# Sample rows' scores against their own new keys: one 128 x 128 product, or four blocks of 32 x 32

## The chip, the cores and the metric

The kernel runs on one core of a Trainium2 chip. The metric is the time of one execution on the device in microseconds (us), the median of several runs; lower is better.

## The reference, cut to what matters

A two-layer trunk is stepped once, for a prompt of 256 tokens and for 8 running streams ("samples") of 16 new tokens each, so 3 blocks of 128 rows. Layer 0 has 8 forgetting-attention heads (fox) and 8 stick-breaking heads (sb), head width 128. A sample's token attends to the 128 cached rows of its own stream and to those of its own 16 new tokens that are not after it:

```python
def fox_core(q, k, v, Fq, Fk, qpos, kpos):
    s = jnp.einsum('bqhd,bkhd->bhqk', q, k).astype(jnp.float32) * ATTN_SCALE
    s = s + (Fq - Fk)          # per head, shapes aligned
    s = jnp.where(kpos[None, :] <= qpos[:, None], s, -jnp.inf)
    p = jax.nn.softmax(s, axis=-1)
    return jnp.einsum('bhqk,bkhd->bqhd', p.astype(v.dtype), v)

def sb_core(q, k, v, qpos, kpos):
    z = jnp.einsum('bqhd,bkhd->bhqk', q, k).astype(jnp.float32) * ATTN_SCALE
    before = kpos[None, :] < qpos[:, None]
    log_stay = jnp.where(before, jax.nn.log_sigmoid(-z), 0.0)
    after = lax.cumsum(log_stay, axis=3, reverse=True) - log_stay
    a = jnp.where(before, jnp.exp(jax.nn.log_sigmoid(z) + after), 0.0)
    return jnp.einsum('bhqk,bkhd->bqhd', a.astype(v.dtype), v)
```

Each head's output is multiplied by a SiLU gate and goes through an output projection to the residual. Layer 1 is a gMLP with spatial gating; the change does not touch it. Everything is float32.

## The kernel before

**Dense projections.** Every large product (`dense_nat`, `products`, L93 to L119) has 128 x 512 tiles of weight streamed from DRAM by the SP queue. ScalarE rounds a tile to a high part (`whi`, L84), VectorE makes the low part by subtraction (`wlo`, L86), and TensorE runs three products for each of the three row blocks (L100, L101, L102). `whi` and `wlo` have four buffers each. The input projection of layer 0 is walked in four "quads" of four heads (`quad(g)`); quads 0 and 1 are fox, 2 and 3 are sb.

**Attention between the dense products.** A head's work is a generator (`head`, L605) that is stepped at fixed places in the dense products of the quad and the next one (`places`, L515, put in through `between`). Heads go in pairs. `scores(pair)` (L480) makes the scores of both heads, runs the softmax or the stick-breaking weights, writes the weights to DRAM (L671, ScalarE's queue) and reads them back in blocks of 32 x 32 moved to their transposed place (L496, GpSimd's queue). `attended(pair)` (L501), one dense product later, turns these blocks with a VectorE transpose (`PT`, L674), multiplies them with the values on TensorE and applies the gate. A tile scheduler orders the instructions of each engine by its own estimate of when they are ready; `tc.issue_after` holds some of them behind others.

**One head on TensorE**, all in float32, where the trace shows one product as two records:
- L630, L631: prompt scores, 128 x 128 stationary.
- L633: sample rows against all 128 new keys of all samples, one 128 x 128 product. A mask of -1e30 leaves each stream its own 16 keys.
- L636: sample rows against cached keys, four products with 32 columns of the array each (32 tokens, 256 cached keys), K = 128.
- L681: sample weights of new keys times new values, four products with K = 128 rows and 32 columns.
- L685: the same for cached values, eight products of that form.
- L687 to L689: prompt weights times values, 128 x 128.

So a sample row has T = 384 weights: 256 for cached keys (two streams' slots) and 128 for new keys. A head's tile `weights` (tag `pr`) holds 384 prompt and 384 sample columns, 768 in all, which is six blocks of 128 in DRAM (`wd`).

**Setup.** L310 to L324 make the masks `mp` (prompt) and `md` (sample) for both kinds of heads. For a fox head L610 to L620 add the forget sums to the masks on GpSimd.

Of the kernel before, what the change touches and what calls it, by code (L numbers as in the profile page):

```python
# [8 lines left out]
F32 = mybir.dt.float32  # L9
F32R = mybir.dt.float32r  # L10
AF = mybir.ActivationFunctionType
ALU = mybir.AluOpType
# [3 lines left out]
P = 128  # L16
# [3 lines left out]
T = NT * P  # L20
# [17 lines left out]
def tile_hybrid_step(  # L38
# [7 lines left out]
    nc = tc.nc  # L46
    V, S, G, PE = nc.vector, nc.scalar, nc.gpsimd, nc.tensor
# [5 lines left out]
    dram = ctx.enter_context(tc.tile_pool(name="dram", bufs=1, space=bass.MemoryType.DRAM))  # L53
# [5 lines left out]
    def nm(s):  # L59
        n_names[0] += 1  # L60
        return f"{s}_{n_names[0]}"

    def slot(dt=F32R):
        return slots.tile([P, 4 * T], dt, tag="slot", name=nm("slot"))
# [91 lines left out]

    with ExitStack() as l0:
        lc = l0.enter_context(tc.tile_pool(name="l0c", bufs=1, reuse_waits="tile"))  # L160
        lp = l0.enter_context(tc.tile_pool(name="l0p", bufs=2, reuse_waits="tile"))
# [126 lines left out]
        def select(ap, pattern, base, cm, fill=0.0, op=ALU.is_ge):  # L288
            G.affine_select(out=ap, in_=ap, pattern=pattern, compare_op=op, fill=fill, base=base, channel_multiplier=cm)
# [20 lines left out]
        for strict in (0, 1):  # L310
            mp = lc.tile([P, T], F32, name=f"mp{strict}")
            V.memset(mp, 0.0)
            for j in (1, 2):
                select(mp[:, j * P:(j + 1) * P], [[-1, P]], -strict, 1, NEG)
            md = lc.tile([P, T], F32, name=f"md{strict}")
            V.memset(md, 0.0)
            for s in range(2):
                with late():
                    V.tensor_scalar(out=md[:, s * P:(s + 1) * P], in0=md[:, s * P:(s + 1) * P], scalar1=slotb[:, s:s + 1], scalar2=None, op0=ALU.add)
            mdn = md[:, 2 * P:].rearrange("p (b q) -> p b q", q=16)  # L320
            select(mdn, [[-16, 8], [0, 16]], 0, 1, NEG)
            select(mdn, [[16, 8], [0, 16]], 15, -1, NEG)
            select(mdn, [[-16, 8], [-1, 16]], -strict, 1, NEG)
            masks.append((mp, md))  # L324


# [5 lines left out]
        nFd = dram.tile([8, T], F32, name="nFd")  # L332
# [135 lines left out]
        def quad(g):  # L468
# [5 lines left out]
            own = {"d": dram.tile([4, T, P], F32, name=nm("d"))}  # L474
# [5 lines left out]
            def scores(pair):  # L480

                for hh in pair:
                    hs = slice(hh * P, hh * P + P)
                    own[hh] = head(g, h0 + hh, own["k"][:, hh], lambda hs=hs: own["v"][:, :, hs], own["q"][:, hh],
                                   keys_of[4 * g + hh], lambda n=4 * g + hh: values_of[n], lambda hs=hs: own["z"][:, :, hs])
                wd = own[pair] = dram.tile([2, 6, P, P], F32, name=nm("wd"))
                for hh in pair[::-1]:
                    next(own[hh])
                with tc.issue_after(last_product[0]):
                    for hh in pair:  # L490
                        next(own[hh])
                for j, hh in enumerate(pair):
                    own[hh].send(wd[j])
                blk = own["blk", pair] = slot(F32).rearrange("p (j x) -> p j x", j=2)
                for j in range(4):
                    G.dma_start(blk[32 * j:32 * j + 32].rearrange("p j (a d) -> p (j a) d", d=32),  # L496
                                wd[:, :, :, 32 * j:32 * j + 32].rearrange("j x (a p) d -> p (j x a) d", p=32))
                for hh in pair:
                    cached_keys(4 * g + hh + 2)
# [78 lines left out]
            for tb in range(NT):  # L578
                z, a = zn[:, tb, :], sg[:, tb, :]
# [22 lines left out]
        def tmp(tag, bufs=2, shape=None):  # L602
            return lp.tile(shape or [P, T], F32, tag=tag, bufs=bufs, name=nm(tag))

        def head(g, h, kT, values, qT, kc, vc, gate):  # L605
            fox = g < 2
            mp, md = masks[0 if fox else 1]
            if fox:

                fb = lp.tile([P, 2, T], F32, tag="fb", name=nm("fb"))  # L610
                fc = lp.tile([P, P], F32, tag="fc", bufs=1, name=nm("fc"))
                G.dma_start(fb[:, 0, :2 * P], nFd[h, :2 * P].partition_broadcast(P))
                G.dma_start(fb[:, 0, 2 * P:], nFd[h, :P].partition_broadcast(P))
                G.dma_start(fb[:, 1, 2 * P:], nFd[h, 2 * P:].partition_broadcast(P))
                G.dma_start(fc, nFcd[:, h, :].unsqueeze(1).broadcast_to([8, 16, P]))
                G.tensor_tensor(out=fb[:, 0, :], in0=fb[:, 0, :], in1=mp, op=ALU.add)
                G.tensor_tensor(out=fb[:, 1, 2 * P:], in0=fb[:, 1, 2 * P:], in1=md[:, 2 * P:], op=ALU.add)
                G.tensor_tensor(out=fb[:, 1, :2 * P].rearrange("p (s k) -> p s k", s=2), in0=md[:, :2 * P].rearrange("p (s k) -> p s k", s=2),
                                in1=fc.unsqueeze(1).broadcast_to([P, 2, P]), op=ALU.add)
                mp, md = fb[:, 0, :], fb[:, 1, :]  # L620

            KTt = []
            for hf in range(2):
# [6 lines left out]
            PE.matmul(sc[:, :2 * P].rearrange("p (t k) -> p t k", t=2), lhsT=qT[:, P:2 * P], rhs=kT[:, :2 * P].rearrange("p (t k) -> p t k", t=2), start=True, stop=True)  # L630
            PE.matmul(sc[:, 2 * P:T], lhsT=qT[:, :P], rhs=kT[:, :P], start=True, stop=True)  # L631
            sd = bank()
            PE.matmul(sd[:, 2 * P:T], lhsT=qT[:, 2 * P:], rhs=kT[:, 2 * P:], start=True, stop=True)  # L633
            wd = yield
            for j in range(4):
                PE.matmul(sd[32 * j:32 * j + 32, :2 * P], lhsT=qT[:, 2 * P + 32 * j:2 * P + 32 * j + 32], rhs=KTt[j // 2][:, (j % 2) * 256:(j % 2) * 256 + 256],  # L636
                          start=True, stop=True)

            weights = lp.tile([P, 2 * T], F32, tag="pr", name=nm("pr"))
            rs = {}  # L640
            for dec, s in ((0, sc), (1, sd)):
                m = md if dec else mp
                blocks = [(0, T, 2)] if dec else [(0, 2 * P, 1), (2 * P, T, 0)]
                z = tmp("z")
                if fox:
                    st = lp.tile([P, 4], F32, tag="st", bufs=8, name=nm("st"))
                    for i, (a, e, tb) in enumerate(blocks):
                        V.scalar_tensor_tensor(out=z[:, a:e], in0=s[:, a:e], scalar=Fnat[:, tb, h:h + 1], in1=m[:, a:e], op0=ALU.add, op1=ALU.add)
                        V.tensor_reduce(out=st[:, i:i + 1], in_=z[:, a:e], axis=AX.X, op=ALU.max, negate=True)
                    pr = weights[:, dec * T:dec * T + T]  # L650
                    for i, (a, e, tb) in enumerate(blocks):
                        S.activation(pr[:, a:e], z[:, a:e], AF.Exp, bias=st[:, i:i + 1], accum_out=st[:, 2 + i:3 + i])
                    n = len(blocks)
                    V.reciprocal(out=st[:, 2:2 + n], in_=st[:, 2:2 + n])
                    for i, (a, e, tb) in enumerate(blocks):
                        rs[tb] = st[:, 2 + i:3 + i]
                else:
                    V.tensor_tensor(out=z, in0=s[:, :T], in1=m, op=ALU.add)
                    l = tmp("l")
                    S.activation(l, z, AF.Abs)  # L660
                    S.activation(l, l, AF.Exp, scale=-1.0)
                    S.activation(l, l, AF.Ln, bias=1.0)
                    V.scalar_tensor_tensor(out=l, in0=z, scalar=0.0, in1=l, op0=ALU.max, op1=ALU.add)
                    for a, e, _ in blocks:
                        V.tensor_tensor_scan(out=l[:, a:e][:, ::-1], data0=ones[:, 0:1].broadcast_to([P, e - a]), data1=l[:, a:e][:, ::-1],
                                             initial=0.0, op0=ALU.mult, op1=ALU.subtract)
                    V.tensor_tensor(out=z, in0=z, in1=l, op=ALU.add)
                    pr = weights[:, dec * T:dec * T + T]
                    S.activation(pr, z, AF.Exp)

            nc.scalar.dma_start(wd.rearrange("x q k -> q x k"), weights.rearrange("q (x k) -> q x k", k=P))  # L671
            blk = yield
            PT = lp.tile([P, 2 * T], F32, tag="PT", name=nm("PT"))
            yield V.transpose(out=PT, in_=blk)  # L674
            PD = PT[:, T:]
            vn, vc, z = values(), vc(), gate()
            ob = bank()
            od, ot = ob[:, 2 * P:3 * P], ob[:, :2 * P]
            for j in range(4):
                js = slice(32 * j, 32 * j + 32)  # L680
                PE.matmul(od[js, :], lhsT=PD[:, 2 * P + 32 * j:2 * P + 32 * j + 32], rhs=vn[:, 2, :], start=True, stop=False)  # L681
            for s in range(2):
                for j in range(4):
                    js = slice(32 * j, 32 * j + 32)
# [329 lines left out]
```

## Time and profile before

| | |
|---|---|
| median of 3 runs | 1794.22 us (1794.20 to 1795.07) |
| profiled execution, own time | 1795.94 us |
| its span, first to last instruction | 1794.2 us |
| TensorE busy | 1782.1 us, 99% |
| VectorE busy | 946.6 us, 53% |
| ScalarE busy | 729.0 us, 41% |
| GpSimd busy | 369.9 us, 21% |

The profile is of one execution. A busy share of TensorE is no measure of how well it is used, since its matmuls overlap in the records; where the time goes is read from when matmuls start. A row of a timeline gives start, duration, engine, line, operation, what it writes and reads, the array's rows*columns, the tile that streams, and how many records are merged ("x16").

### The profile page before, as it was taken

The page shows a single profiled execution, that of the slowest core. Times are in us where ns is not written, and L with a number is a line of the kernel's source. Part 1 is how long each engine was busy: PE and PEld are TensorE (multiplying, and loading weights), DVE is VectorE, ACT ScalarE, POOL GpSimd, SP SyncE. Part 2 cuts the span into 40 slices and gives each one's busy share as a digit, 9 for nine tenths or more (in the row PEclk, how much of TensorE's full clock was granted, in tenths as well). Part 3 has the DMA queues.
Part 4 walks back from the last instruction along what each step waited for, and adds up shares of the span by engine and source line. Part 5 has one row for each costly group of instructions (what it writes and reads, how often), then busy time and mean ns, then how long its engine had stood idle before and what let it go on. Part 6 is the DMA issues. An engine that isn't in the chain of part 4 may idle for free.

```text
span 1794.2 us, 24567 instructions
## 1 busy us (share of the span) xinstructions
PE 1782.1 (99%) x8623; PEld 1480.1 (82%) x8623; DVE 946.6 (53%) x1578; ACT 729.0 (41%) x1301; POOL 369.9 (21%) x544
## 2 busy tenths in 40 slices
PE   9999999999999999999999999999999999999998
PEld 8988878888888888888888888888888888888887
DVE  6437465457448455534434556455555464455366
ACT  5435354346337344433333333433333333433344
POOL 1516544223311211200300121220120210220020
PEclk9999999999999999999999999999999999999999
DMA  6868988868867877644444454454454554455553
GB/s 198 248 172 212 273 225 225 236 176 227 234 189 196 236 198 195 190 129 130 137 130 124 144 158 128 145 147 148 145 147 116 151 156 129 146 146 150 156 146 119
DMA packets 185772, 307.64 MB, mean 171 GB/s; under 512 B 22904, under 2 KB 63152, under 8 KB 185648
## 3 DMA queue, kind: packets, MB, share of 16 engines
q1 hardware_dynamic: 127696, 225.37, 42.6%
q0 software_dynamic: 25072, 63.53, 14.0%
q10 hardware_dynamic: 32880, 17.18, 3.2%
q8 instruction: 67, 1.10, 0.3%
q14 instruction: 57, 0.47, 0.1%
HBM read 269.23 MB, written 30.47 MB: 167 GB/s over the span
## 4 chain that ended last, share of the span: by engine, by line
PE 95%; DMA 2%; issue 1%; DVE 1%; POOL 1%; ACT 0%; POOLq 0%; DVEq 0%; ACTq 0%
PE d L100 29%; PE d L102 29%; PE d L101 29%; DMA slot<-in_sgu_ln_b_dram 1%; PE a L101 1%; PE a L100 1%; PE a L102 1%; DMA d<-gz 0%; PE a L636 0%; DMA slot<-d 0%; PE a L630 0%; PE a L886 0%; PE d L426 0%; PE a L685 0%; PE d L944 0%
## 5 line engine op out<-in xcount | busy, mean ns | idle before, releaser
L86 DVE TENSOR_TENSOR wlo<-raw,whi 128x512 fp32r<-128x512 f32 x784 | 538.9, 696 | 722.2 <-ACT whi L84 721.9
L101 PE MATMUL d<-wlo,slot 128*128 128x512 f32 x2349 | 912.1, 390 | 1.7 <-DVE wlo L86 1.7
L102 PE MATMUL d<-whi,slot 128*128 128x512 f32 x2349 | 911.5, 389 | 0.0
L84 ACT ACTIVATE whi<-raw 128x512 fp32r<-128x512 f32 x784 | 493.1, 631 | 900.7 <-PE d L102 838.2
L100 PE MATMUL d<-whi,slot 128*128 128x512 f32 x2349 | 822.4, 390 | 0.0
L101 PEld LDWEIGHTS d<-wlo,slot 128*128 128x128 f32 x2349 | 441.0, 188 | 93.7 <-DVE wlo L86 3.2
L100 PEld LDWEIGHTS d<-whi,slot 128*128 128x128 f32 x2349 | 440.6, 188 | 93.9 <-issue 0.8
L102 PEld LDWEIGHTS d<-whi,slot 128*128 128x128 f32 x2349 | 440.9, 188 | 91.1
L128 POOL DMA_DIRECT2D gTt<-trn x128 | 77.9, 617 | 315.1 <-issue 190.1
L398 POOL DMA_DIRECT2D slot<-d x48 | 44.0, 923 | 140.8 <-DVE wlo L86 54.6
L837 POOL DMA_DIRECT2D wr<-in_w_sp_dram x64 | 34.9, 552 | 113.1 <-DVE wT L841 99.0
L496 POOL DMA_DIRECT2D slot<-wd x32 | 29.3, 922 | 103.5 <-DMA wd<-pr 41.1
L830 DVE TENSOR_TENSOR slot<-d,slot 128x512 f32<-128x512 f32 x48 | 32.4, 689 | 13.8 <-PE d L102 13.8
L786 POOL DMA_DIRECT2D slot<-in_sgu_ln_g_dram x8 | 4.6, 569 | 133.4 <-PE d L102 133.4
L457 POOL DMA_DIRECT2D kcache<-in_cache_sb_k_dram x32 | 24.9, 785 | 32.6 <-DVE KT L625 32.6
L457 POOL DMA_DIRECT2D kcache<-in_cache_fox_k_dram x32 | 25.0, 787 | 22.1 <-DVE KT L625 20.9
L712 POOL DMA_DIRECT2D blk<-h1d x12 | 10.9, 918 | 70.3 <-DMA h1d<-slot 59.9
L802 POOL DMA_DIRECT2D bcol<-in_b_sp_dram x1 | 1.2, 1176 | 116.1 <-DVE w L801 116.1
L780 POOL TENSOR_SCALAR rsv<-mvr 128x3 f32<-128x3 f32 x1 | 0.5, 538 | 108.1 <-DVE mvr L779 108.1
L777 DVE BATCH_NORM_STATS2 stats<-vt 128x6 f32<-128x512 f32 x24 | 16.2, 689 | 11.6 <-ACT vt L776 11.6
L865 DVE SCALAR_TENSOR_TENSOR gate<-d,rstd,gate 128x512 f32<-128x512 f32 x24 | 17.4, 749 | 7.3 <-PE d L102 7.3
L862 ACT ACTIVATE gate<-d,rstd 128x512 f32<-128x512 f32 x24 | 16.5, 689 | 11.2 <-PE d L102 11.1
(247 smaller groups left out, 1270.9 us busy)
## 6 DMA issues: line engine op xcount, KB each, us to landing
raw<-in_w_in_dram SPq DMA_DIRECT2D x640, 256.0 KB, 2.8
raw<-in_w_out_dram SPq DMA_DIRECT2D x189, 256.0 KB, 3.3
slot<-d POOLq DMA_DIRECT2D x48, 192.0 KB, 5.7
d<-slot ACTq DMA_DIRECT2D x24, 256.0 KB, 3.7
wd<-pr ACTq DMA_DIRECT2D x16, 384.0 KB, 5.7
slot<-wd POOLq DMA_DIRECT2D x32, 192.0 KB, 5.8
gTt<-trn POOLq DMA_DIRECT2D x128, 48.0 KB, 3.5
kcache<-in_cache_fox_k_dram POOLq DMA_DIRECT2D x32, 128.0 KB, 5.9
```

Source lines behind the costliest of these rows:

```text
L84: highs.append(S.activation(hi, raw, AF.Copy).ins)
L86: splits.append(V.tensor_tensor(out=lo, in0=raw, in1=f32(hi), op=ALU.subtract).ins)
L100: PE.matmul(o, lhsT=his[k][:, t], rhs=hi[:, 0, :], start=(k == first), stop=False)
L101: PE.matmul(o, lhsT=his[k][:, t], rhs=lo[:, 0, :], start=False, stop=False)
L102: mm = PE.matmul(o, lhsT=los[k][:, t], rhs=hi[:, 0, :], start=False, stop=(k == last))
L128: G.dma_start(dst[32 * j:32 * j + 32, :, 32 * a:32 * a + 32], trn[32 * a:32 * a + 32, :, 32 * j:32 * j + 32])
L398: r = G.dma_start(blk[32 * j:32 * j + 32].rearrange("p h (a d) -> p (h a) d", d=32), d[:, :, 32 * j:32 * j + 32].rearrange("h (a p) d -> p ...
L457: G.dma_start(k[32 * j:32 * j + 32].rearrange("p (b d) -> p b d", d=32), (c_fox_k, c_sb_k)[n // 8][:, :, n % 8, 32 * j:32 * j + 32].rearra ...
L496: G.dma_start(blk[32 * j:32 * j + 32].rearrange("p j (a d) -> p (j a) d", d=32), wd[:, :, :, 32 * j:32 * j + 32].rearrange("j x (a p) d -> ...
L830: evicted = V.tensor_tensor(out=h1[c][:, tb, :], in0=o[tb], in1=h1[c][:, tb, :], op=ALU.add)
L837: G.dma_start(wr[js, 0, :].rearrange("p (a s) -> p a s", s=32), w_sp[g, :, js].rearrange("(a p) s -> p a s", p=32))
L865: V.scalar_tensor_tensor(out=gate[:, tb, :], in0=o[tb], scalar=rstd[:, tb:tb + 1], in1=gate[:, tb, :], op0=ALU.mult, op1=ALU.mult)
```

## The change

The sample scores against new keys become blocks: tokens 32j to 32j+31 (two streams) against keys 32j to 32j+31 alone, four products of 32 x 32 with K = 128. A sample row then has 288 columns (256 cached, 32 new) through mask, softmax and cumulative sum. These 32 last columns are not sent through DRAM: a VectorE transpose, which turns each 32 x 32 block in place, makes `own` from them, and the product with the new values uses K = 32 rows and 32 columns, four blocks on the diagonal of the array. `wd` has five blocks of 128 in place of six.

```diff
+    TW = 2 * P + 32
-            md = lc.tile([P, T], F32, name=f"md{strict}")
+            md = lc.tile([P, TW], F32, name=f"md{strict}")
...
-            mdn = md[:, 2 * P:].rearrange("p (b q) -> p b q", q=16)
+            new = lp.tile([P, 2 * T], F32, tag="PT", name=nm("new"))[:, :P]
+            V.memset(new, 0.0)
+            mdn = new.rearrange("p (b q) -> p b q", q=16)
...
+            for j in range(4):
+                js = slice(32 * j, 32 * j + 32)
+                G.tensor_copy(md[js, 2 * P:], new[js, js])
...
-                wd = own[pair] = dram.tile([2, 6, P, P], F32, name=nm("wd"))
+                wd = own[pair] = dram.tile([2, 5, P, P], F32, name=nm("wd"))
...
-                G.dma_start(fb[:, 1, 2 * P:], nFd[h, 2 * P:].partition_broadcast(P))
+                G.dma_start(fb[:, 1, 2 * P:TW], nFd[h, 2 * P:].rearrange("(j k) -> j k", k=32).unsqueeze(1).broadcast_to([4, 32, 32]))
...
-            PE.matmul(sd[:, 2 * P:T], lhsT=qT[:, 2 * P:], rhs=kT[:, 2 * P:], start=True, stop=True)
             wd = yield
+            for j in range(4):
+                js = slice(2 * P + 32 * j, 2 * P + 32 * j + 32)
+                PE.matmul(sd[32 * j:32 * j + 32, 2 * P:TW], lhsT=qT[:, js], rhs=kT[:, js], start=True, stop=True)
...
-            weights = lp.tile([P, 2 * T], F32, tag="pr", name=nm("pr"))
+            weights = lp.tile([P, T + TW], F32, tag="pr", name=nm("pr"))
...
-                blocks = [(0, T, 2)] if dec else [(0, 2 * P, 1), (2 * P, T, 0)]
+                blocks = [(0, TW, 2)] if dec else [(0, 2 * P, 1), (2 * P, T, 0)]
...
-            nc.scalar.dma_start(wd.rearrange("x q k -> q x k"), weights.rearrange("q (x k) -> q x k", k=P))
+            nc.scalar.dma_start(wd.rearrange("x q k -> q x k"), weights[:, :5 * P].rearrange("q (x k) -> q x k", k=P))
+            own = lp.tile([P, 32], F32, tag="own", bufs=4, name=nm("own"))
+            V.transpose(out=own, in_=weights[:, 5 * P:])
...
-            PT = lp.tile([P, 2 * T], F32, tag="PT", name=nm("PT"))
+            PT = lp.tile([P, 2 * T], F32, tag="PT", name=nm("PT"))[:, :5 * P]
...
-                PE.matmul(od[js, :], lhsT=PD[:, 2 * P + 32 * j:2 * P + 32 * j + 32], rhs=vn[:, 2, :], start=True, stop=False)
+                PE.matmul(od[js, :], lhsT=own[js, :], rhs=vn[js, 2, :], start=True, stop=False)
```

## Rows read from the trace of the kernel before

**Rows 1.** The page: busy time, share of the span and instructions of each engine (PEld is TensorE's weight load).

```profile
PE 1782.1 (99%) x8623; PEld 1480.1 (82%) x8623; DVE 946.6 (53%) x1578; ACT 729.0 (41%) x1301; POOL 369.9 (21%) x544
```

**Rows 2.** The page: the chain of work that ended last, shares of the span by engine.

```profile
PE 95%; DMA 2%; issue 1%; DVE 1%; POOL 1%; ACT 0%; POOLq 0%; DVEq 0%; ACTq 0%
```

**Rows 3.** Waits of TensorE over the whole span, the largest of four lines: who waited for whom, us in total, times, longest.

```profile
PE d L101 <- DVE wlo L86: 1.7, 3, 1.3
...
```

**Rows 4.** Timeline of TensorE at the end of the scores of a pair of sb heads.

```profile
395.63 0.38 PE L631 MATMUL a<-kT,qT 128*128 128x128 f32 x2
395.86 0.39 PE L633 MATMUL a<-kT,qT 128*128 128x128 f32 x2
396.17 1.07 PE L636 MATMUL a<-KT,qT 128*32 128x256 f32 x16
397.17 0.50 PE L100 MATMUL d<-whi,slot 128*128 128x512 f32 x1
397.51 0.39 PE L101 MATMUL d<-wlo,slot 128*128 128x512 f32 x1
397.74 0.39 PE L102 MATMUL d<-whi,slot 128*128 128x512 f32 x1
```

**Rows 5.** Timeline of TensorE through the `attended` part of a pair; seven of the eight have this order.

```profile
209.71 0.39 PE L100 MATMUL d<-whi,slot 128*128 128x512 f32 x1
210.02 0.43 PE L681 MATMUL a<-vnat,PT 128*32 128x128 f32 x8
210.27 0.62 PE L685 MATMUL a<-vcache,PT 128*32 128x128 f32 x16
210.70 0.40 PE L681 MATMUL a<-vnat,PT 128*32 128x128 f32 x8
210.92 0.62 PE L685 MATMUL a<-vcache,PT 128*32 128x128 f32 x16
211.47 0.49 PE L687 MATMUL a<-vnat,PT 128*128 128x128 f32 x2
211.80 0.39 PE L688 MATMUL a<-vnat,PT 128*128 128x128 f32 x2
```

**Rows 6.** The same of the first pair, where the second head's part comes after a product of the first.

```profile
179.34 0.49 PE L687 MATMUL a<-vnat,PT 128*128 128x128 f32 x2
179.76 0.43 PE L681 MATMUL a<-vnat,PT 128*32 128x128 f32 x8
```

**Rows 7.** Timeline of TensorE at the forget sums: products that all use the same 8 columns of the array, of one and of 128 streamed columns, and a product on 8 rows of the array.

```profile
71.27 0.54 PE L364 MATMUL a<-ones,clf 128*8 128x1 f32 x16
71.67 1.91 PE L374 MATMUL a<-sums,clf 128*8 128x128 f32 x16
73.51 0.39 PE L426 MATMUL d<-whi,slot 128*128 128x256 f32 x1
...
79.80 0.28 PE L427 MATMUL d<-wlo,slot 128*128 128x256 f32 x1
79.92 0.28 PE L428 MATMUL d<-whi,slot 128*128 128x256 f32 x1
80.13 0.35 PE L383 MATMUL a<-ident,FT 8*128 8x8 f32 x3
```

**Rows 8.** Timeline of TensorE's weight loads, the first of an `attended` part: eight loads, from the first one's start to the last one's end.

```profile
178.55 0.16 PEld L681 LDWEIGHTS a<-vnat,PT 128*32 128x32 f32 x8 [0.35 <-issue]
```

**Rows 9.** VectorE by line and shape from 130 to 610 us: busy time, mean ns of one, idle time before.

```profile
L674 DVE STREAM_TRANSPOSE PT<-slot 128x768 f32<-128x768 f32 x16 | 14.7, 955 | 0.9 <-DMA slot<-wd 0.9
L665 DVE TENSOR_TENSOR_SCAN l<-ones,l 128x384 f32<-128x384 f32 x8 | 7.6, 952 | 0.1
L665 DVE TENSOR_TENSOR_SCAN l<-ones,l 128x256 f32<-128x256 f32 x8 | 5.5, 688 | 0.1
```

**Rows 10.** Waits of VectorE, then of ScalarE (both from 60 to 610 us), then of GpSimd (from 0 to 610 us).

```profile
DVE wlo L86 <- ACT whi L84: 199.4, 121, 3.6
DVE st L654 <- ACT pr L652: 1.0, 2, 0.9
ACT whi L84 <- PE d L102: 227.9, 99, 5.8
POOL wf L340 <- DVE wf L337: 24.6, 1, 24.6
```

**Rows 11.** Timeline of TensorE and of VectorE at its longest wait.

```profile
236.31 0.39 PE L100 MATMUL d<-whi,slot 128*128 128x512 f32 x1
237.99 0.50 PE L101 MATMUL d<-wlo,slot 128*128 128x512 f32 x1 [1.30 <-DVE wlo L86]
235.58 1.78 DVE L594 STREAM_TRANSPOSE vnat<-slot 128x1536 f32<-128x1536 f32 x1 [4.97 <-DMA slot<-d]
```

**Rows 12.** Timelines of VectorE, ScalarE and TensorE after the last scores of a pair of sb heads.

```profile
561.26 0.56 DVE L667 TENSOR_TENSOR z<-z,l 128x384 f32<-128x384 f32 x1
561.74 1.29 DVE L86 TENSOR_TENSOR wlo<-raw,whi 128x512 fp32r<-128x512 f32 x2
562.03 0.51 ACT L669 ACTIVATE pr<-z 128x384 f32<-128x384 f32 x1
563.49 0.51 ACT L669 ACTIVATE pr<-z 128x384 f32<-128x384 f32 x1
563.97 0.39 PE L101 MATMUL d<-wlo,slot 128*128 128x512 f32 x1
```

More of the change, by code (lines that the diff above doesn't have):

```diff
@@ L493, in scores @@
                     own[hh].send(wd[j])
-                blk = own["blk", pair] = slot(F32).rearrange("p (j x) -> p j x", j=2)
+                blk = own["blk", pair] = slot(F32)[:, :2 * 5 * P].rearrange("p (j x) -> p j x", j=2)
                 for j in range(4):
@@ L613, in head @@
                 G.dma_start(fb[:, 0, 2 * P:], nFd[h, :P].partition_broadcast(P))
-                G.dma_start(fb[:, 1, 2 * P:], nFd[h, 2 * P:].partition_broadcast(P))
+                G.dma_start(fb[:, 1, 2 * P:TW], nFd[h, 2 * P:].rearrange("(j k) -> j k", k=32).unsqueeze(1).broadcast_to([4, 32, 32]))
                 G.dma_start(fc, nFcd[:, h, :].unsqueeze(1).broadcast_to([8, 16, P]))
                 G.tensor_tensor(out=fb[:, 0, :], in0=fb[:, 0, :], in1=mp, op=ALU.add)
-                G.tensor_tensor(out=fb[:, 1, 2 * P:], in0=fb[:, 1, 2 * P:], in1=md[:, 2 * P:], op=ALU.add)
+                G.tensor_tensor(out=fb[:, 1, 2 * P:TW], in0=fb[:, 1, 2 * P:TW], in1=md[:, 2 * P:], op=ALU.add)
                 G.tensor_tensor(out=fb[:, 1, :2 * P].rearrange("p (s k) -> p s k", s=2), in0=md[:, :2 * P].rearrange("p (s k) -> p s k", s=2),
                                 in1=fc.unsqueeze(1).broadcast_to([P, 2, P]), op=ALU.add)
-                mp, md = fb[:, 0, :], fb[:, 1, :]
+                mp, md = fb[:, 0, :], fb[:, 1, :TW]
             KTt = []
@@ L642, in head @@
                 m = md if dec else mp
-                blocks = [(0, T, 2)] if dec else [(0, 2 * P, 1), (2 * P, T, 0)]
-                z = tmp("z")
+                blocks = [(0, TW, 2)] if dec else [(0, 2 * P, 1), (2 * P, T, 0)]
+                n = TW if dec else T
+                z = tmp("z")[:, :n]
+                pr = weights[:, dec * T:dec * T + n]
                 if fox:
@@ L649, in head @@
                         V.tensor_reduce(out=st[:, i:i + 1], in_=z[:, a:e], axis=AX.X, op=ALU.max, negate=True)
-                    pr = weights[:, dec * T:dec * T + T]
                     for i, (a, e, tb) in enumerate(blocks):
                         S.activation(pr[:, a:e], z[:, a:e], AF.Exp, bias=st[:, i:i + 1], accum_out=st[:, 2 + i:3 + i])
-                    n = len(blocks)
-                    V.reciprocal(out=st[:, 2:2 + n], in_=st[:, 2:2 + n])
+                    V.reciprocal(out=st[:, 2:2 + len(blocks)], in_=st[:, 2:2 + len(blocks)])
                     for i, (a, e, tb) in enumerate(blocks):
@@ L657, in head @@
                 else:
-                    V.tensor_tensor(out=z, in0=s[:, :T], in1=m, op=ALU.add)
-                    l = tmp("l")
+                    V.tensor_tensor(out=z, in0=s[:, :n], in1=m, op=ALU.add)
+                    l = tmp("l")[:, :n]
                     S.activation(l, z, AF.Abs)
@@ L667, in head @@
                     V.tensor_tensor(out=z, in0=z, in1=l, op=ALU.add)
-                    pr = weights[:, dec * T:dec * T + T]
                     S.activation(pr, z, AF.Exp)
-            nc.scalar.dma_start(wd.rearrange("x q k -> q x k"), weights.rearrange("q (x k) -> q x k", k=P))
+            nc.scalar.dma_start(wd.rearrange("x q k -> q x k"), weights[:, :5 * P].rearrange("q (x k) -> q x k", k=P))
+            own = lp.tile([P, 32], F32, tag="own", bufs=4, name=nm("own"))
+            V.transpose(out=own, in_=weights[:, 5 * P:])
             blk = yield
-            PT = lp.tile([P, 2 * T], F32, tag="PT", name=nm("PT"))
+            PT = lp.tile([P, 2 * T], F32, tag="PT", name=nm("PT"))[:, :5 * P]
             yield V.transpose(out=PT, in_=blk)
```

## The prediction, made before the changed kernel was run

> **What bounds the kernel now.** I read the page's busy times first, then the chain, then TensorE's waits, and last the timelines of the three places that the change touches. TensorE is at 99% of the span, VectorE at 53% [rows 1]; the chain that ends last is TensorE for 95% [rows 2]. That alone could still hide waits, so the waits decide: over the whole span TensorE waits 1.7 us for a low part of a weight tile, in three places [rows 3], and 1.3 us of it is one place [rows 11]. So the time is the sum of what TensorE is given to do, at a pace of 0.23 us for a dense product (L101 to L102 in [rows 4]). Whatever the change takes from VectorE, ScalarE, GpSimd or the DMA queues is worth nothing by itself, except at that one wait. What it does to TensorE's order counts in full.
>
> **Scores: what goes.** L633 is one float32 product of 128 x 128. Its twin L631 takes 0.23 us from its start to the next (395.63 to 395.86) [rows 4]. With 0.225 us for each of 16 heads, 3.6 us go. L633 stood right before L636, so its move to behind the second step changes no neighbour.
>
> **Scores: what comes.** Four products, eight records, with 32 streamed columns, on the four strips of 32 array columns that L636 then uses; no change of form is added. Eight records of such a form with 128 columns take 0.22 us (L681 at 210.70 to L685 at 210.92), so four strips run side by side, since 16 records in one and the same strip take 1.84 us, 0.115 us each [rows 5, 7]. In proportion 32 columns need 0.055 us. Against it stands the cost of issuing a record: 16 products of one streamed column take 0.40 us, 0.025 us each, but in one strip [rows 7]; eight would be 0.20 us. Eight loads in four strips start and end within 0.16 us [rows 8], so strips do not wait for one another at that pace. I take 0.06 us, by L681, which has the same strips; the ends are 0.055 and 0.20. Saved: 16 x (0.225 - 0.06) = 2.6 us, at least 0.4, at most 2.7.
>
> The Trainium skill, "TensorE: Matmul & The Clock Gate", Part 1, says that starts never come closer than about 25 ns, however few columns stream. By that the eight records would take 0.20 us and the whole forecast would be 2.2 us later, at 1796.3. No run here shows short products in several strips, and L681's 0.22 us for eight agrees with either.
>
> **Attended: the same product, but a change of form.** L681 has 128 rows x 32 columns of the array; its successor has 32 x 32. If four diagonal blocks run side by side, they take the 0.22 us of L681. But L685 behind them stays at 128 rows. What a change of form costs is in the rows. Into the strips: L100 to L681 is 0.31 us, 0.08 over the pace, and the first L681 takes 0.25 where the second takes 0.22: 0.11 us together [rows 5]. Back to the full array: the second L685 takes 0.55 us where 16 records at L681's rate are 0.44, and the first L687 takes 0.33 where 0.22 is its due: 0.22 us [rows 5]. A change of rows alone costs too: L428 to L383, which has 8 rows, is 0.21 us where L427 to L428 is 0.12 [rows 7]. Before, a pair has one way in and one way out, since the second head's L681 follows L685 at once. After, it has L684 to L685, L685 to the second head's L684, and L684 to L685 again: three more. I take 0.11 us each, as for a way into narrow strips, which 32 columns are on both sides. Seven pairs with three, and the first pair, which goes back to the full array in its middle [rows 6], with two: 23 x 0.11 = 2.5 us. The ends are nothing (if the strips need no stop when only the rows change) and 23 x 0.22 = 5.1 us.
>
> The Trainium skill, "TensorEngine Tiling (Array Packing)", Tiling Modes, Key Properties, has the rule that a change of tiling mode drains TensorE, and 128 x 32 and 32 x 32 are two modes there. The rows at the ways in and out agree with it, at 0.11 and 0.22 us; that it also holds between these two no row shows.
>
> **Work that is covered.** VectorE: `PT` goes from 768 to 640 columns, 0.16 us less by its 955 ns; the scan over 96 columns fewer is 0.20 us less by 952 and 688 ns [rows 9]; the other sample operations shrink alike, and `own` adds one small transpose. ScalarE's exponentials shrink too. Both engines wait for others: VectorE 199 us for high parts, ScalarE 228 us for TensorE to free buffers [rows 10]. So this is worth nothing now; without that cover it would be a gain of a few us, not a cost. DRAM traffic of the weights falls by a sixth, which only shortens a round trip that ends well ahead of its use. The eight new copies of the masks' diagonal blocks, and the selects that move to another tile, are on GpSimd in the first microseconds; it then waits 24.6 us for VectorE before it issues its first load [rows 10], so the copies cost nothing; without that wait they would delay loads that are needed tens of us later. The new-key mask of a fox head is still one DMA at the same place of GpSimd's queue, and its addition gets smaller.
>
> **A new wait.** `own` reads what ScalarE's last exponential writes, so VectorE can stand still for ScalarE, with splits of weights queued behind it and TensorE behind those. The nearest row is fox's reciprocal, which has the same wait: 1.0 us in two places of the whole layer [rows 10], and TensorE waits at none of them. After fox's reciprocal the new wait is none. For sb heads I take 0: the scheduler puts an instruction where it reckons it ready. The upper end is a rival below.
>
> **Sum.** -2.6 + 2.5 = -0.1 us on the profiled execution's own 1795.94 us (1.7 us of it outside the span), so 1795.8. The median of the runs is 1.7 us under that execution, which makes 1794.1 us. By the ends alone: 1794.2 - 2.7 = 1791.5, and 1794.2 - 0.4 + 5.1 = 1798.9.
>
> **Rivals.**
> - *The change of rows costs nothing* (0.15). For it: the column strips stay the same. Against it: L383, where a change of rows cost 0.09 us [rows 7]. Time: 1794.2 - 2.6 = 1791.6; with the one long wait of 1.45 us gone too (1.68 us between starts less the pace, [rows 11]) it is 1790.1. That wait hangs on a DMA for a VectorE transpose, which a lighter load may bring sooner.
> - *The diagonal blocks run one after the other* (0.13), the case on the other side. All four write to one bank of PSUM, and no row here has four strips of rows at work. Then eight records cost what L374's do, 0.115 us each, 0.92 in place of 0.22 us [rows 7]: 16 x 0.70 = 11.2 us, 1805.3. It decides from the point where they need more than 0.45 us in place of 0.22. The Trainium skill, "TensorEngine Tiling (Array Packing)", Gotcha 1: PSUM Pressure, states that different row tiles cannot access the same PSUM bank at one time, which would give this; no run here shows it yet. Against it: each block writes other partitions, as L681's strips do, which share a bank and overlap.
> - *`own` holds up VectorE* (0.15). In [rows 12] the second head's last exponential ends at 564.00. If `own` stood ahead of the two splits at 561.74, they would start 2.3 us later; the second ends at 563.03, 0.9 us before the L101 at 563.97. So TensorE would lose about 1.4 us at a pair, from a delay of 0.9 us on. With two to four sb pairs: 1797 to 1800.
> - *The offset as summed* (0.57): 1794.1, its own range 1792 to 1797.5.
>
> 0.2% is 3.6 us, about what a measurement of this kernel tells from no change: faster means under 1790.6, slower over 1797.8. Faster needs free changes of rows and the long wait gone: 0.05. Slower: the serial blocks 0.13, most of the third rival 0.10, the upper end of the changes of form 0.03, so 0.26. Same: 0.69. The range 1791 to 1800 leaves out the serial blocks and the lower tail of the first rival, under 0.2.
>
> **What will show it.** In the score part: L636's predecessor missing, and from the last 128 x 128 product to L636's end about 0.33 us less for a pair (two heads' 0.165). In the attended part: from the dense product before to L687 about 0.33 us more for a pair, with gaps of 0.1 us at each change of rows; the four blocks starting together or 0.1 us apart tells the second rival at once. In the waits: TensorE's for low parts should stay near 1.7 us; if it grows by some us between 390 and 610 us, `own` did it. The forecast is wrong if the scheduler orders a pair otherwise (more or fewer changes of form), or if a low part comes late.

## The result, and the profile after

The changed kernel takes 1797.47 us (median of 17 runs, 1796.58 to 1799.51), the kernel before 1794.53 us beside it (17 runs, 1793.72 to 1799.44): the medians are 2.9 us apart. The ratio, estimated from all runs of both with a 95% interval, is 1.0018 [1.0012, 1.0025]: 3.2 us more, from 2.2 to 4.5. The forecast was no change to within 0.1 us, with a range that holds 1797.5. The loss is small, but it is outside what the runs leave open, and it has a cause.

The page after, and below it all waits of TensorE over the whole span (us in total, times, longest):

```profile
PE 1784.9 (99%) x8719; PEld 1476.8 (82%) x8719; DVE 940.9 (52%) x1596; ACT 725.9 (40%) x1301; POOL 370.0 (21%) x552
```

```profile
PE a L201 <- DVE ones L134: 1.1, 1, 1.1
PE a L899 <- DVE vl L91: 0.5, 3, 0.2
PE d L256 <- DVE slot L231: 0.4, 1, 0.4
```

VectorE, ScalarE and DMA got less to do, and TensorE is at 99% as in [rows 1]. Its waits for low parts of weights, 1.7 us in [rows 3], are gone from this profile, and nothing waits for `own`. So the 3 us are neither a new wait nor an engine that became the bound: TensorE itself spends more time between the same dense products. Lines have shifted: L631 is now L640, the new scores are L645, L636 is L647, L681 is L694, L685 is L698, L687 to L689 are L700 to L702.

The scores of the pair of [rows 4], TensorE's timeline; the first line is the pair's first score product before, the others are after:

```profile
394.33 0.59 PE L630 MATMUL a<-kT,qT 128*128 128x256 f32 x2
```

```profile
394.62 0.59 PE L639 MATMUL a<-kT,qT 128*128 128x256 f32 x2
...
395.71 0.38 PE L640 MATMUL a<-kT,qT 128*128 128x128 f32 x2
396.02 0.27 PE L645 MATMUL a<-kT,qT 128*32 128x32 f32 x8
396.10 0.62 PE L647 MATMUL a<-KT,qT 128*32 128x256 f32 x8
396.54 0.24 PE L645 MATMUL a<-kT,qT 128*32 128x32 f32 x8
396.60 0.62 PE L647 MATMUL a<-KT,qT 128*32 128x256 f32 x8
397.15 0.50 PE L100 MATMUL d<-whi,slot 128*128 128x512 f32 x1
397.48 0.39 PE L101 MATMUL d<-wlo,slot 128*128 128x512 f32 x1
```

Eight records of the new form take 0.08 us (396.02 to 396.10) and 0.06 us (396.54 to 396.60) where L633 took 0.225. From a pair's first score product to the second dense product behind it, it was 3.18 us (394.33 to 397.51) and is now 2.86 (394.62 to 397.48): 0.32 less, 2.56 for eight pairs.

An `attended` part as the forecast thought of it, against [rows 5]:

```profile
445.61 0.42 PE L694 MATMUL a<-vnat,own 32*32 32x128 f32 x8
445.96 0.64 PE L698 MATMUL a<-vcache,PT 128*32 128x128 f32 x16
446.53 0.42 PE L694 MATMUL a<-vnat,own 32*32 32x128 f32 x8
446.88 0.64 PE L698 MATMUL a<-vcache,PT 128*32 128x128 f32 x16
447.45 0.49 PE L700 MATMUL a<-vnat,PT 128*128 128x128 f32 x2
447.78 0.39 PE L701 MATMUL a<-vnat,PT 128*128 128x128 f32 x2
...
449.13 0.40 PE L102 MATMUL d<-whi,slot 128*128 128x512 f32 x1
```

The second dense product behind the part of [rows 5], before:

```profile
213.15 0.39 PE L102 MATMUL d<-whi,slot 128*128 128x512 f32 x1
```

L694 to L698 is now 0.35 us, where 0.22 was L681's; L698 to the second L694 is 0.57, where 16 records at that rate are 0.44. So each change between the forms 32*32 and 128*32 costs 0.13 us, and the eight records of four diagonal blocks still take 0.22. Three such changes make the part, from its first product to the second dense product behind it, 3.52 us (445.61 to 449.13) instead of 3.12 (210.02 to 213.15).

What the forecast did not have is elsewhere, far ahead of the `attended` parts. TensorE's timeline some 17 us ahead of the second pair's:

```profile
189.18 0.39 PE L102 MATMUL d<-whi,slot 128*128 128x512 f32 x1
189.50 0.40 PE L694 MATMUL a<-vnat,own 32*32 32x128 f32 x2
189.83 0.50 PE L100 MATMUL d<-whi,slot 128*128 128x512 f32 x1
190.26 0.41 PE L694 MATMUL a<-vnat,own 32*32 32x128 f32 x4
190.60 0.50 PE L101 MATMUL d<-wlo,slot 128*128 128x512 f32 x1
...
191.95 0.40 PE L694 MATMUL a<-vnat,own 32*32 32x128 f32 x2
...
199.32 0.42 PE L694 MATMUL a<-vnat,own 32*32 32x128 f32 x8
...
206.93 1.10 PE L698 MATMUL a<-vcache,PT 128*32 128x128 f32 x32
```

And the fourth pair:

```profile
312.93 0.39 PE L102 MATMUL d<-whi,slot 128*128 128x512 f32 x1
313.25 0.40 PE L694 MATMUL a<-vnat,own 32*32 32x128 f32 x2
313.58 0.96 PE L100 MATMUL d<-whi,slot 128*128 128x512 f32 x3
314.38 0.40 PE L101 MATMUL d<-wlo,slot 128*128 128x512 f32 x1
...
317.88 0.41 PE L694 MATMUL a<-vnat,own 32*32 32x128 f32 x6
318.22 0.64 PE L698 MATMUL a<-vcache,PT 128*32 128x128 f32 x16
```

Products with `own` (L694) stand alone between dense products, in groups of two, four or eight records, and every group pays a way into the narrow form and one back. For the two records at 313.25: from L102 at 312.93 to L101 at 314.38 are 1.45 us, where four dense products (L102 and three L100) are 0.91; 0.54 us, of which the two records' own work is an estimated 0.06, a quarter of the 0.22 for eight. VectorE's timeline shows when the inputs were there for the second pair, the later of its two `own` and both `PT`:

```profile
182.13 0.19 DVE L684 STREAM_TRANSPOSE own<-pr 128x32 f32<-128x32 f32 x1
...
201.75 1.57 DVE L687 STREAM_TRANSPOSE PT<-slot 128x640 f32<-128x640 f32 x2 [0.97 <-DMA slot<-wd]
```

L681 read `PT`, so nothing of a pair could be placed ahead of that transpose. L694 reads `own`, which is there 20 us earlier, and the values, which the first pair's products read from the same tile at 177.94. The source asks for the order with `tc.issue_after(turned[...])`, which ties instructions to others of the same engine; `turned` are VectorE instructions, so it never held a product of TensorE: L694 runs at 189.50, ahead of the transposes at 201.75 that it was to follow. The data did. Only the second, fourth, sixth and eighth pair lose work in this way; why the scheduler moves these and leaves the others, no run shows.

Against the kernel before, worked out from both timelines (us; for an early group, from the dense product ahead of it to the second behind it, less the dense pace):

| | us |
|---|---|
| scores, 8 pairs by -0.32 | -2.56 |
| `attended` part, 7 pairs by +0.40, and the first +0.07 | +2.87 |
| early groups of pairs 4, 6 and 8, net +0.53 each | +1.58 |
| early groups of pair 2, net | +1.34 |
| sum | +3.2 |

From the first score product to the second dense product after the last `attended` part, before takes 466.40 us, 464.85 without its one long wait of [rows 11] (1.55 us with the start after it), and after 468.00: 3.15 us more, as the sum says to within 0.1. This stretch, called the attention stretch below, leaves out what comes ahead of the first scores, where profiles of these kernels differ by up to 1.9 us.

### The profile page after: what moved, and what is told of

Read it like the earlier page. It is cut to its first block, busy times and chain, and to the rows that moved or that the text cites. A ratio compares the mean times of both kernels' runs of the same rounds, so it can differ in the third digit from the quotient of the medians.

```text
span 1795.4 us, 24790 instructions
## 1 busy us (share of the span) xinstructions
PE 1784.9 (99%) x8719; PEld 1476.8 (82%) x8719; DVE 940.9 (52%) x1596; ACT 725.9 (40%) x1301; POOL 370.0 (21%) x552
## 5 line engine op out<-in xcount | busy, mean ns | idle before, releaser
L101 PE MATMUL d<-wlo,slot 128*128 128x512 f32 x2349 | 911.7, 390 | 0.0
L102 PE MATMUL d<-whi,slot 128*128 128x512 f32 x2349 | 911.1, 389 | 0.0
L100 PE MATMUL d<-whi,slot 128*128 128x512 f32 x2349 | 822.6, 390 | 0.0
L100 PEld LDWEIGHTS d<-whi,slot 128*128 128x128 f32 x2349 | 440.4, 188 | 94.8 <-issue 2.4
L101 PEld LDWEIGHTS d<-wlo,slot 128*128 128x128 f32 x2349 | 441.1, 188 | 91.3 <-DVE wlo L86 0.9
L102 PEld LDWEIGHTS d<-whi,slot 128*128 128x128 f32 x2349 | 441.0, 188 | 90.9
L789 ACT ACTIVATE vt<-d,rstd 128x512 f32<-128x512 f32 x24 | 16.4, 690 | 13.3 <-PE d L102 13.3
L634 DVE STREAM_TRANSPOSE KT<-kcache 128x512 f32<-128x512 f32 x32 | 19.7, 674 | 3.1 <-DMA kcache<-in_cache_fox_k_dram 1.8
```

The source lines that it names most:

```text
L100: PE.matmul(o, lhsT=his[k][:, t], rhs=hi[:, 0, :], start=(k == first), stop=False)
L101: PE.matmul(o, lhsT=his[k][:, t], rhs=lo[:, 0, :], start=False, stop=False)
L102: mm = PE.matmul(o, lhsT=los[k][:, t], rhs=hi[:, 0, :], start=False, stop=(k == last))
L634: V.transpose(out=t, in_=kc[:, hf * 4 * P:(hf + 1) * 4 * P])
```

## The experiments

The theory (A): the loss is the early groups, 2.9 us, on top of changes of form of 0.13 us each, and the score blocks earn their 2.6 us. Rivals: the early groups fill time that was to be spent anyway, so holding them back gives nothing (B); the 32-row products are dear in themselves and not through the changes of form around them (C); more small transposes for `own` hold up VectorE and through it TensorE (D). The first four kernels ran beside one median of before, 1795.42 us (32 runs, 1792.76 to 1798.25), the last four beside another, 1794.35 us (33 runs, 1793.45 to 1799.58). An interval of these ratios is about 3.2 us wide, so the medians can tell 3 us from nothing, but hardly kernels that lie 1 to 2 us apart; for these the attention stretch of the profiled execution is read. Where the same products run in the same order it comes out alike: 468.00 us in both profiles of the changed kernel, 461.89 in those of the fifth experiment and the seventh, and 464.79 in the sixth beside 464.85 worked out for before.

**Held behind the dense product.** The products with `own` get an order on their own engine.

```diff
-                with tc.issue_after(turned[0].ins), tc.issue_after(turned[1].ins):
+                with tc.issue_after(turned[0].ins), tc.issue_after(turned[1].ins), tc.issue_after(last_product[0]):
```

> The changed kernel with one addition: TensorE's instructions of an attended part are queued behind the last dense product before its place, so the products with own can no longer be issued several us early. Theory A (early products, each between two changes of form, cost about 2.8 us of the 5.8 us that the attended parts lost): pairs 4, 6 and 8 lose their early product (0.51 us each), the second pair keeps one excursion in place of four, so 1795.3 where before is 1794.5 and the changed kernel 1797.4. Rival B (the loss is the three more changes of form in each burst, or VectorE's new transposes): no change, 1797.4.

Measured: 1794.40 us, ratio 0.9997 [0.9988, 1.0006]. 0.8 us over before was expected. The interval lies wholly under the changed kernel's [1.0012, 1.0025]; the attention stretch is 464.92 us, 3.1 less than after. So the early groups were the loss, and B falls. One is left, ahead of the second pair:

```profile
197.37 0.39 PE L102 MATMUL d<-whi,slot 128*128 128x512 f32 x1
197.69 0.64 PE L694 MATMUL a<-vnat,own 32*32 32x128 f32 x16
198.26 0.50 PE L100 MATMUL d<-whi,slot 128*128 128x512 f32 x1
```

The hold ties to the last dense product traced before, and here `own` was still ready long before `PT`. The scores and `attended` parts with this group sum to +0.3 us against before, and the stretch gives +0.07; the remaining 0.2 us is spread over the some 1,800 steps between dense products, at 0.1 ns each, and not explained.

**Held, and own of both heads together.** The cached products of both heads come first, then the own products of both: two changes of form fewer per pair, and the order hangs on products that do need `PT`.

```diff
...
+                    cached = [next(own[hh]) for hh in pair]
+                with tc.issue_after(cached[0].ins), tc.issue_after(cached[1].ins):
...
-            for j in range(4):
-                js = slice(32 * j, 32 * j + 32)
-                PE.matmul(od[js, :], lhsT=own[js, :], rhs=vn[js, 2, :], start=True, stop=False)
...
+                    cached = PE.matmul(od[js, :], lhsT=PD[:, s * P + 32 * j:s * P + 32 * j + 32], rhs=vc[:, 2 * j + s, :], start=(s == 0), stop=False)
+            yield cached
+            for j in range(4):
+                js = slice(32 * j, 32 * j + 32)
+                PE.matmul(od[js, :], lhsT=own[js, :], rhs=vn[js, 2, :], start=False, stop=True)
```

> As e1_held, and the order within a pair is turned: cached values of both heads first, then own values of both heads, so a pair has one more change of form than before in place of three. Theory A with 0.13 us a change between narrow strips (0.40 us a burst over three): 16 changes fewer than with three, 2.1 us less than e1_held apart from the excursion of the second pair (0.5 us), which goes too: 1793.0, faster than before by 1.5 us. Rival C (a burst is longer because blocks of 32 rows run slower, whatever the order): as e1_held, 1795.3, less 0.5 at most.

Measured: 1792.69 us, 0.9990 [0.9981, 0.9999]; stretch 463.38.

```profile
302.66 0.39 PE L102 MATMUL d<-whi,slot 128*128 128x512 f32 x1
302.98 1.08 PE L697 MATMUL a<-vcache,PT 128*32 128x128 f32 x32
303.99 0.64 PE L701 MATMUL a<-vnat,own 32*32 32x128 f32 x16
304.56 0.49 PE L703 MATMUL a<-vnat,PT 128*128 128x128 f32 x2
```

The 32 cached records are due 0.88 us by the rate of [rows 5] and take 1.01, the 16 own ones 0.44 and take 0.57 with their way out: one change of form, again 0.13 us, in place of three. The part is 3.25 us in seven pairs, 0.13 over before, with the same 32-row products (the first pair is split by three dense products). So it is the changes and not the products that cost, and C falls.

**Held, own on all 128 rows.** `own` becomes a 128 x 128 tile, zero but for the diagonal blocks, which four small transposes write; its product has K = 128 and the form 128*32 of its neighbours, so that no change of form is left to save.

```diff
...
+        own_blocks = [lc.tile([P, P], F32, name=f"own{i}") for i in range(4)]
...
-            own = lp.tile([P, 32], F32, tag="own", bufs=4, name=nm("own"))
-            V.transpose(out=own, in_=weights[:, 5 * P:])
+            own = own_blocks[(4 * g + h) % 4]
+            for j in range(4):
+                js = slice(32 * j, 32 * j + 32)
+                V.transpose(out=own[js, js], in_=weights[js, 5 * P:])
...
-                PE.matmul(od[js, :], lhsT=own[js, :], rhs=vn[js, 2, :], start=True, stop=False)
+                PE.matmul(od[js, :], lhsT=own[:, js], rhs=vn[:, 2, :], start=True, stop=False)
...
```

This kernel also has the hold of the first experiment, zeroes the four tiles once, and gives the tiles of `PT` 640 columns in place of 768; so do the fifth and the seventh.

> As e1_held, but own is a 128 x 128 tile with four 32 x 32 blocks on its diagonal and zeros elsewhere (four small transposes a head), so the product with own values has K = 128 rows as before and no change of rows is left. Theory A: the saving of the scores stands alone, -2.6 us, plus 0.5 us for the one excursion of the second pair: 1792.4. Rival D (VectorE's transposes that wait for ScalarE's exponential cost the time): slower than e1_held, since there are four transposes a head in place of one, 1796 or more.

Measured: 1793.24 us, 0.9990 [0.9981, 0.9999]; stretch 462.60, 2.25 less than before. VectorE's timeline at one head, then TensorE's:

```profile
291.84 0.83 DVE L690 STREAM_TRANSPOSE own<-pr 32x32 f32<-32x32 f32 x4
```

```profile
301.43 0.43 PE L700 MATMUL a<-vnat,own 128*32 128x128 f32 x8
301.67 0.62 PE L704 MATMUL a<-vcache,PT 128*32 128x128 f32 x16
302.11 0.40 PE L700 MATMUL a<-vnat,own 128*32 128x128 f32 x8
302.33 0.62 PE L704 MATMUL a<-vcache,PT 128*32 128x128 f32 x16
302.88 0.49 PE L706 MATMUL a<-vnat,PT 128*128 128x128 f32 x2
```

Spacing for spacing these are [rows 5], and the part is 3.12 us again. Four transposes take 0.83 us where one took 0.19, 10 us more of VectorE's time over 16 heads, and TensorE waits for no low part and for no `own` in this profile: D falls. The second pair's own products still run alone, all 16 records at 197.44, as in the first experiment.

**The old scores.** The kernel before with the `attended` half alone, held as in the first experiment. The scores, their mask and softmax stay 128 keys wide, and four small transposes take the diagonal blocks out of them.

```diff
...
-            nc.scalar.dma_start(wd.rearrange("x q k -> q x k"), weights.rearrange("q (x k) -> q x k", k=P))
+            nc.scalar.dma_start(wd.rearrange("x q k -> q x k"), weights[:, :5 * P].rearrange("q (x k) -> q x k", k=P))
+            own = lp.tile([P, 32], F32, tag="own", bufs=4, name=nm("own"))
+            for j in range(4):
+                js = slice(32 * j, 32 * j + 32)
+                V.transpose(out=own[js, :], in_=weights[js, 5 * P + 32 * j:5 * P + 32 * j + 32])
...
```

It also has the hold, the five blocks in DRAM, and the product with `own` of the changed kernel.

> The kernel before with the attended half of the change alone: scores and softmax over 384 columns with one 128 x 128 product, own made by four small transposes of the diagonal blocks, K = 32 products, five blocks through DRAM; attended parts held as in e1_held. Theory A: +0.40 us for seven bursts, 0.1 for the first, 0.5 for the excursion: 1794.5 + 3.4 = 1797.9, so 2.6 us over e1_held. If the narrower scores and softmax save nothing on TensorE: as e1_held.

Measured: 1798.36 us, 1.0021 [1.0012, 1.0030], 2.9 us over before by the medians and 3.8 by the ratio. It is 4.0 over the median of the first experiment, from which it differs by the scores, their wider softmax, and four small transposes in place of one. Its bursts are 3.18 us for the scores, as before, and 3.52 for `attended`, as after, with one early group as in the first experiment. So one half of the change is a gain and the other a loss. The profiled execution is the longest of its runs (1801.78 us). It has the wait of [rows 11] at the same place, longer; the first line is VectorE's, the others are TensorE's:

```profile
235.19 1.78 DVE L594 STREAM_TRANSPOSE vnat<-slot 128x1536 f32<-128x1536 f32 x1 [7.01 <-DMA slot<-d]
237.60 0.80 PE L101 MATMUL d<-wlo,slot 128*128 128x512 f32 x1 [2.55 <-DVE wlo L86]
238.19 0.63 PE L102 MATMUL d<-whi,slot 128*128 128x512 f32 x1
238.61 0.63 PE L100 MATMUL d<-whi,slot 128*128 128x512 f32 x1
```

Its stretch is 471.80 us, and 467.7 without the 4.1 us that this wait and the slow products behind it take. That is 2.9 over before, what its bursts sum to, and 2.8 over the first experiment, where the scores alone are 2.56. So the size of each half rests on the traces; the medians show its sign.

**Full rows, queued behind the cached products.** The third experiment with the own products last, each head's tied to its cached ones, so that neither an early group nor a split of the first pair is possible.

```diff
...
+                    cached = PE.matmul(od[js, :], lhsT=PD[:, s * P + 32 * j:s * P + 32 * j + 32], rhs=vc[:, 2 * j + s, :], start=(s == 0), stop=False)
+            with tc.issue_after(cached.ins):
+                for j in range(4):
+                    js = slice(32 * j, 32 * j + 32)
+                    PE.matmul(od[js, :], lhsT=own[:, js], rhs=vn[:, 2, :], start=False, stop=True)
```

> As e3_held_full_rows (own with zeros around its four blocks, K = 128), and own's products are queued behind the cached values of their head, so that the last early product goes too. Theory A: the saving of the scores, 8 x 0.32 = 2.6 us, and nothing against it: 2.6 us under the kernel before, 0.5 us under e3_held_full_rows; with the first pair in one piece another 0.3 us. If the narrower scores were worth less: the same as e3_held_full_rows.

Measured: 1792.40 us, 0.9989 [0.9980, 0.9998]; stretch 461.89, 0.7 under the third experiment and 2.96 under before. Of this the scores are 2.56, and 0.34 comes about because the first pair now runs in one piece, where [rows 6] had a product of the full array (L687) between its heads.

**Before, with the wait at 236 us taken away.** The forecast took 1.7 us off the profiled execution to reach the median, and that profile held a wait of 1.3 us. To see whether the wait is what sets executions apart, the first `mix_split`, whose load and transpose stand at that place, comes four steps later in the dense product.

```diff
-            at(g + 1, *(("z", 4) if g == 0 else ("q", 8)), lambda: mix_split())
+            at(g + 1, *(("z", 8) if g == 0 else ("q", 8)), lambda: mix_split())
```

> The kernel before, with the first mix_split put at the ninth step of quad 1's gate projection in place of the fifth, so that VectorE's transpose of that block no longer stands in its queue before its DMA has landed. Tests the base of the forecast: the profiled execution of before had a wait of 1.45 us there. If it is in some executions and not in others, the spread of the kernel before (1793 to 1798) shrinks towards its lower end and the median falls by 0.5 to 1.5 us; if the wait is no cause of the spread, both stay.

Measured: 1794.47 us (1793.94 to 1796.20), 1.0001 [0.9992, 1.0010]. The wait is gone from the profile, whose span is 1792.7 us and whose stretch is 464.8, but the median is that of before, and 11 runs still spread over 2.3 us. The profiled execution, which has no such wait, itself takes 1794.45 us, as long as the median of before. So the median of before does not seem to hold the wait, and what spreads its executions over several microseconds stays open. Profiles also differ before the first score product, which no run here took apart.

**Both together.** The fifth and sixth edits in one kernel.

> e5_full_rows_behind_cached and e6_before_mix_later together: the saving of the scores and the first mix_split later. If the two are independent: e6_before_mix_later less 2.6 us, about 3 to 4 us under the kernel before.

Measured: 1791.53 us (1790.47 to 1793.64), 0.9984 [0.9975, 0.9993]: 2.8 us under before, the fastest of all. Its stretch is 461.89, the same as without the move, so the 0.9 us between the two medians are within what these runs can tell.

In the third pair's `attended` part TensorE goes from its first cached product at 300.89 to the first of the full array at 302.34: the 1.45 us of [rows 5] (210.02 to 211.47), in one form from the way in to the way out.

**The changed kernel again,** unedited, beside these.

> The changed kernel itself, beside the others on one chip. Theory A: 3 us over the kernel before and 5.5 us over e5_full_rows_behind_cached (2.8 us early products, 2.9 us changes of form).

Measured: 1798.58 us, 1.0017 [1.0008, 1.0027]; stretch 468.00, with the same early groups. By the medians it is 4.2 us over before, by the ratio 3.1. 6.2 us (5.5 expected) lie between it and the fifth experiment, which computes the same with `own` on full rows and in its place.

## Why the prediction missed

- **What bounds the kernel: right.** All that moved the time is TensorE's sequence. VectorE lost 5.7 us and later got 10 us more without a trace in the end.
- **Scores: right.** 0.06 us for a head's four products was forecast by L681, 0.06 to 0.08 measured; 2.56 us saved against 2.6. The upper bound of 0.20, from one strip's spacing in [rows 7], was far off. The text held that L681's 0.22 us agrees with either rate; L681's single records do not, since the first four, one in each strip, start within 0.02 us (178.55 to 178.57).
- **Changes of form: right in kind, a little low.** 0.13 us each against 0.11 taken from the ways in of [rows 5]. The first pair was to keep its split and have two changes; it ran in one piece with three, 0.07 us longer than before. In all 2.87 us against 2.5.
- **The step that failed** is "After, it has L684 to L685, L685 to the second head's L684, and L684 to L685 again: three more." (Its L684 stands for the product with `own`, L694 in the trace after, and its L685 for L698.) That is right where a pair keeps its order, but the step took the order of [rows 5] as given and asked only what the changes in it cost. But that order was held by data, by `PT`, and the change put the product on `own`, ready 20 us before. The part on VectorE asked whether `own` might be late; nobody asked what comes early. Four of eight pairs lost work out of the part, seven groups with a way in and out each, 2.9 us, where the sum had nothing. That is nearly the whole miss of 3.3 us on the sum (changes of form make the other 0.4). Held behind a dense product in the first experiment, these products gave the attention stretch 3.1 us back. The text's last sentence named an order with more changes of form as a way to be wrong, but gave it no price and no chance. The rows to price it were there: 0.11 for a way in and 0.22 back [rows 5], and for seven groups 2.3 us.
- **The rivals: none came.** Changes of rows cost 0.13, not nothing. The four blocks ran side by side (0.22 us for eight records). `own` held up no engine: TensorE has no wait for a low part after the change, and no transpose to `own` waits for ScalarE. That the time fell into the third rival's 1797 to 1800 is chance; its mechanism is in no trace.
- **From the execution to the median.** The 1.7 us taken off gave 1794.2, and the runs of before give 1794.35 to 1795.42, so the base was good enough. That the profiled execution's wait was about as long invited a reason that the sixth experiment does not support.

## What to carry to other kernels

When a change replaces the input of an instruction by one that is ready earlier, find out what held that instruction in its place until now. If it was data, and the written order names another engine's instructions, a scheduler may now put it anywhere before; tie it to an instruction of its own engine, here the last cached product.
Here small products paid for their form more than for their size. Padding `own` with zeros to the form of its neighbours cost TensorE nothing and gave back 0.40 us a pair, where a quarter of the rows had saved nothing.

## What the hardware showed that was not expected

Records that stream 32 columns in four different strips follow one another at a mean of 8 to 10 ns (eight in 0.06 to 0.08 us), while records in one strip stand 25 ns apart with a single column [rows 7]. The Trainium skill, "TensorE: Matmul & The Clock Gate", Part 1, has starts never closer than about 25 ns, which would make eight 0.20 us; the trace does not agree where the records lie in several strips, and the measurement decides.

Four diagonal blocks of 32*32, each on other rows and other partitions of one PSUM tile, overlap as fully as four column strips do: eight records in 0.22 us and 16 in 0.44, both with the 0.13 of one change of form taken off. The Trainium skill, "TensorEngine Tiling (Array Packing)", Gotcha 1: PSUM Pressure, says that different row tiles cannot access one bank at the same time; here, with each block on partitions of its own, no such delay is seen. The rule of the Trainium skill, "TensorEngine Tiling (Array Packing)", Tiling Modes, Key Properties, that a change of tiling mode drains TensorE, does agree: between 128*32 and 32*32 a change cost 0.13 us wherever a head's eight records stood together.

The fourth experiment's long wait has a second cost. Busy time of each engine in three stretches around it (behind the window its length; in a column the busy time, then its records; PEclk is the granted clock):

```profile
core 0: us, PE busy (x) PEld busy (x) DVE busy (x) ACT busy (x) POOL busy (x), PEclk, DMA share, GB/s
230.00:234.00 4.00, 4.00 (x20) 3.30 (x19) 0.00 (x0) 0.91 (x2) 0.00 (x0) 1.00 0.97 275
237.60:240.30 2.70, 2.70 (x6) 2.17 (x7) 2.70 (x6) 2.21 (x5) 2.36 (x3) 0.50 0.77 218
241.00:245.00 4.00, 4.00 (x20) 3.29 (x19) 1.61 (x3) 1.27 (x2) 0.00 (x0) 1.00 1.03 265
```

After standing for 2.55 us TensorE was granted 0.50 of its clock, 1.2 GHz in place of 2.4, and of the six dense products there the first took 0.59 us to the next start and the others 0.43 each, instead of 0.23, which adds 1.4 us to the wait. After the wait of 1.30 us in [rows 11] the granted clock is 1.00 (237.99 to 240.30 us) and the products run at their usual pace.
